# Row standard deviations on one core: the first group in eight transfers of 16 partitions, and four smaller changes to a kernel's two ends

## The chip, the core and the metric

The kernel runs on one core of a Trainium2 chip. Its time is the device time of one execution in microseconds (us), taken as the median of several executions. The profile of one execution has a span, from the first to the last instruction that the profiler saw; it is 1.7 to 2.1 us shorter than the device time. Engines are called TensorE, VectorE (DVE in the profile), ScalarE (ACT), GpSimdE (POOL) and SyncE (SP, which here only waits and issues transfers). "DMA engines" are the sixteen that move data between HBM and the on-chip memory SBUF.

## The reference

```python
def setup_inputs():
    return {"x": np.random.randn(8192, 8192).astype(np.float32)}

def reference(x):
    return np.std(x, axis=1)
```

The input has 268.4 MB, the output 32 KB. Every element is read once, so the load of x is the floor: at the 433.5 GB/s that the stream reaches below it is 619 us, an estimate (268.4 MB over that rate).

## The kernel before

The 8192 rows are cut into 30 groups of 256 rows and a tail of 512. A group is one transfer: partition p receives rows 2p and 2p+1, 64 KB in one piece, 8.39 MB in all. Three buffers are used in turn. For each group VectorE sums each row while ScalarE squares and sums it; the last groups and the tail are shared between the two engines by columns, so that the work left after the last byte is short. The last block of 128 rows arrives in pieces of columns.

```python
    pieces = [(3072, 768), (1536, 1024), (1024, 0), (1024, 512), (512, 0), (512, 0), (512, 0)]
    ...
    for g in range(G):                                            # G = 30
        if g >= NBUF:
            nc.sync.wait_ge(free, g - NBUF + 1)
        nc.sync.dma_start(out=buf[g % NBUF], in_=xg[g]).then_inc(lane[g % NBUF], 16)
    ...                                                           # the tail's transfers
    for g in range(G - 1):
        nc.vector.wait_ge(*landed(g))
        v_group.append(V.did(nc.vector.reduce_sum(                # row sums
            out=s_all[:, 2 * g:2 * g + 2],
            in_=buf[g % NBUF].rearrange("p (j m) -> p j m", j=2), axis=AX)))
    ...                                                           # ScalarE: squares
    shared(B0, ...); shared(B0 + 1, ...); shared(2 * G, ...)      # bn_stats + bn_aggr on VectorE
    ...
    q_groups = joined(vN[:, B0:2 * G], B0, 2 * G)                 # nine small GpSimdE operations
    ...
    aggregated(fin[:, 0:2], tri)                                  # the last block
    v_fin = V.did(nc.vector.transpose(out=tr, in_=fin[:, 1:33]))
    A.did(nc.scalar.activation(out=std_l, in_=tr, func=ACTF.Sqrt))
    A.need(A, A.n)
    nc.scalar.dma_start(out=out_l, in_=std_l[0:P:32, :]).then_inc(done_l, 16)
```

`landed(g)` is the semaphore value at which group g has arrived; every transfer adds 16.

Of the kernel before, what the change touches and what calls it, by code (L numbers as in the profile page):

```python
# [9 lines left out]
ALU = mybir.AluOpType  # L10
# [4 lines left out]
@with_exitstack  # L15
def kernel(
    ctx: ExitStack,
    tc: tile.TileContext,
    x: bass.AP,
    out: bass.AP,  # L20
):

    ctx.enter_context(tc.tile_critical())  # L23
    std_kernel(ctx, tc.nc, x, out)


def std_kernel(ctx, nc, x, out):
    P = nc.NUM_PARTITIONS
    R, C = x.shape
    N = float(C)  # L30
# [5 lines left out]
    TR = 4  # L36
    G = (R // P - TR) // 2
    B0 = 2 * (G - 1)
    T0 = 2 * G * P
    xg = x[0:T0, :].rearrange("(g p j) m -> g p (j m)", g=G, p=P, j=2)  # L40
    xt_rows = x[T0:R, :].rearrange("(t p) m -> t p m", p=P)
# [3 lines left out]
    out_l = out[T0:T0 + P].rearrange("(b i) -> b i", b=4)  # L45
    ACT_ROW = 3072
    N_D = float(C - ACT_ROW)
    H = C // 2
    pieces = [(3072, 768), (1536, 1024), (1024, 0), (1024, 512), (512, 0), (512, 0), (512, 0)]

    def sb(name, shape, dt=FP32):
        return ctx.enter_context(nc.sbuf_tensor(name, shape, dt))[:]

    def sem(name):
        return ctx.enter_context(nc.semaphore(name))

    NBUF = 3
    buf = [sb(f"x{i}", [P, 2 * C]) for i in range(NBUF)]

    dump = sb("dump", [P, C], mybir.dt.uint8)  # L60
    s_all = sb("s_all", [P, 2 * G + TR])
    q_all = sb("q_all", [P, 2 * G + TR])
    half = sb("half", [P, 2])
    agg = sb("agg", [P, 2 * G + TR - 1 - B0, 2])
    ident = sb("ident", [P, P])
    cinv = sb("cinv", [P, 1])
    nd = sb("nd", [P, 1])
    vN = sb("vN", [P, 2 * G])
    m2 = sb("m2", [P, 2 * G])
    u = sb("u", [P, TR])  # L70
    w = sb("w", [P, TR])
    t3 = sb("t3", [P, TR - 1])
    warm = sb("warm", [P, 1])

# [2 lines left out]
    std_l = sb("std_l", [P, 32])  # L77
# [24 lines left out]
    V = Line(nc.vector, "v")  # L102
    A = Line(nc.scalar, "a")
    Q = Line(nc.gpsimd, "q")
    T = Line(nc.tensor, "t")
    free, token, row_done, squared = sem("free"), sem("token"), sem("row_done"), sem("squared")
    lane = [sem(f"lane{i}") for i in range(NBUF)]
    NT = 4 + len(pieces)
    tail = [sem(f"tail{i}") for i in range(NT)]
    done_g, done_t, done_l = sem("done_g"), sem("done_t"), sem("done_l")  # L110

    def landed(g):
        return lane[g % NBUF], 16 * (g // NBUF + 1)

    xl, xa, xb = (buf[k % NBUF] for k in (G - 1, G, G + 1))



# [1 line left out]
        eng.addr_align(128, offset=0, max_nops=0)  # L120


    for g in range(G):
        if g >= NBUF:
            nc.sync.wait_ge(free, g - NBUF + 1)
        nc.sync.dma_start(out=buf[g % NBUF], in_=xg[g]).then_inc(lane[g % NBUF], 16)  # L126
    nc.sync.wait_ge(free, G - NBUF + 1)
    for i, t in enumerate((1, 2)):
        nc.sync.dma_start(out=xa[:, i * C:(i + 1) * C], in_=xt_rows[t]).then_inc(tail[i], 16)
    nc.sync.wait_ge(free, G - NBUF + 2)  # L130
    for h in range(2):
        nc.sync.dma_start(out=xb[:, h * H:(h + 1) * H],  # L132
                          in_=xt_rows[3][:, h * H:(h + 1) * H]).then_inc(tail[2 + h], 16)
    c0 = 0
    for i, (n, _) in enumerate(pieces):
        nc.sync.dma_start(out=xb[:, C + c0:C + c0 + n],
                          in_=xt_rows[0][:, c0:c0 + n]).then_inc(tail[4 + i], 16)
        c0 += n


    def q_op(op, *args, **kw):
        Q.need(Q, Q.n)
        return Q.did(op(*args, **kw))  # L143

    q_warm = Q.did(nc.gpsimd.memset(warm, 1.0))
    Q.did(nc.gpsimd.memset(ident, 1.0))
    q_op(nc.gpsimd.affine_select, out=ident, in_=ident, compare_op=ALU.is_equal,
                   fill=0.0, base=0, pattern=[[-1, P]], channel_multiplier=1)
    Q.did(nc.gpsimd.memset(cinv, 1.0 / N))
    Q.did(nc.gpsimd.memset(nd, N_D))  # L150
# [5 lines left out]
    v_group = []  # L156
    for g in range(G - 1):
        nc.vector.wait_ge(*landed(g))
        v_group.append(V.did(nc.vector.reduce_sum(  # L159
            out=s_all[:, 2 * g:2 * g + 2],  # L160
            in_=buf[g % NBUF].rearrange("p (j m) -> p j m", j=2), axis=AX)))

    def squash(src, n, func, acc, scale=1.0):
        A.need(A, A.n)
        return nc.scalar.activation(out=dump[:, 0:n], in_=src, func=func, scale=scale, accum_out=acc)  # L165
# [15 lines left out]
    for g in range(LOOPS * NBUF, G - 1):  # L181
        nc.scalar.wait_ge(*landed(g))
        for j in range(2):
            a_group[g] = A.did(squash(buf[g % NBUF][:, j * C:(j + 1) * C], C, ACTF.Square,
                                      q_all[:, 2 * g + j:2 * g + j + 1]))
    a_groups = A.n


    for g in range(G - 1):
        if g < LOOPS * NBUF:  # L190
            nc.tensor.wait_ge(*landed(g))
            nc.tensor.nop().then_inc(token, 1)
        T.need(V, v_group[g])
        if g in a_group:
            T.need(A, a_group[g])
        else:
            nc.tensor.wait_ge(squared, g + 1)
        nc.tensor.nop().then_inc(free, 1)  # L198


    def bn_cols(bn, k, src):
        n = src.shape[1]
        for d0 in range(0, n, F):
            V.did(nc.vector.bn_stats(out=bn[:, k * SD:(k + 1) * SD], in_=src[:, d0:min(n, d0 + F)]))  # L204
            k += 1
        return k

    def aggregated(out_ap, bn):
        V.need(V, V.n)
        return V.did(nc.vector.bn_aggr(out=out_ap, in_=bn))  # L210

    def shared(r, parts):
        bn = bns[r % 2]
        k = 0
        for i, (src, arrived) in enumerate(parts):
            a = ACT_ROW // len(parts)
            qa, sa = (q_all[:, r:r + 1], s_all[:, r:r + 1]) if i == 0 else (half[:, 1:2], half[:, 0:1])
            nc.scalar.wait_ge(*arrived)
            A.did(squash(src[:, 0:a], a, ACTF.Square, qa))
            A.did(squash(src[:, 0:a], a, ACTF.Copy, sa))  # L220
            nc.vector.wait_ge(*arrived)
            k = bn_cols(bn, k, src[:, a:src.shape[1]])
        aggregated(agg[:, r - B0, :], bn)

    def joined(out_ap, r0, r1):
        n = r1 - r0
        ndb = nd.to_broadcast((P, n))
        cb = cinv.to_broadcast((P, n))
        dm, dv = agg[:, r0 - B0:r1 - B0, 0], agg[:, r0 - B0:r1 - B0, 1]
        u_, w_ = u[:, 0:n], w[:, 0:n]  # L230
        q_op(nc.gpsimd.tensor_mul, u_, dm, dm)
        q_op(nc.gpsimd.tensor_add, u_, u_, dv)
        q_op(nc.gpsimd.tensor_mul, u_, u_, ndb)
        q_op(nc.gpsimd.tensor_add, u_, u_, q_all[:, r0:r1])
        q_op(nc.gpsimd.tensor_mul, w_, dm, ndb)
        q_op(nc.gpsimd.tensor_add, w_, w_, s_all[:, r0:r1])
        q_op(nc.gpsimd.tensor_mul, w_, w_, w_)
        q_op(nc.gpsimd.tensor_mul, w_, w_, cb)
        return q_op(nc.gpsimd.tensor_sub, out_ap, u_, w_)

    last = landed(G - 1)
    shared(B0, [(xl[:, 0:C], last)])
    shared(B0 + 1, [(xl[:, C:2 * C], last)])
    v_pair, a_pair = V.n, A.n
    shared(2 * G, [(xa[:, 0:C], (tail[0], 16))])


    Q.need(V, v_group[-1])
    Q.need(A, a_groups)
    q_op(nc.gpsimd.tensor_mul, m2[:, 0:B0], s_all[:, 0:B0], s_all[:, 0:B0])  # L250
    q_op(nc.gpsimd.tensor_mul, m2[:, 0:B0], m2[:, 0:B0], cinv.to_broadcast((P, B0)))
    q_op(nc.gpsimd.tensor_sub, vN[:, 0:B0], q_all[:, 0:B0], m2[:, 0:B0])
    Q.need(V, v_pair)
    Q.need(A, a_pair)
    q_groups = joined(vN[:, B0:2 * G], B0, 2 * G)


    vg = vN.rearrange("p (g j) -> p g j", j=2)
    T.need(Q, q_groups)
    for j in range(2):  # L260
        T.did(nc.tensor.transpose(ps_g[:, j, :], vg[:, :, j], ident))  # L261
    shared(2 * G + 1, [(xa[:, C:2 * C], (tail[1], 16))])
# [12 lines left out]
    c0, k, j = C, 0, 0  # L275
    for i, (n, a) in enumerate(pieces):
        src = xb[:, c0:c0 + n]
# [18 lines left out]
        k = bn_cols(tri[:, 3 * n_act:], k, src[:, a:n])  # L296
# [9 lines left out]
    v_fin = V.did(nc.vector.transpose(out=tr, in_=fin[:, 1:33]))  # L306
    A.need(V, v_fin)
    A.did(nc.scalar.activation(out=std_l, in_=tr, func=ACTF.Sqrt))  # L308
    A.need(A, A.n)
    nc.scalar.dma_start(out=out_l, in_=std_l[0:P:32, :]).then_inc(done_l, 16)  # L310
    nc.sync.wait_ge(done_g, 16)
    nc.sync.wait_ge(done_t, 16)
    nc.sync.wait_ge(done_l, 16)
# [30 lines left out]
```

## Time and profile before

| | before |
|---|---|
| median device time | 631.03 us (630.95 to 631.23, 3 runs) |
| span of the profile | 629.2 us |
| first transfer issued | 1.01 us |
| first row sum starts (group 0 has landed) | 23.41 us |
| one group to the next, landing to landing | 19.35 us (433.5 GB/s) |
| one row sum on VectorE | 17.22 us |
| last piece landed, last store landed | 624.02, 627.56 us |

The first lines are from the profile's page. The first two rows give the span in 40 equal slices: the busy tenths of the DMA engines (9 is 90% or more) and the GB/s that they moved. The third is the load queue: packets, MB, share of the sixteen engines' span.

```profile
DMA  9999999999999999999999999999999999999996
GB/s 401 400 467 400 467 400 467 400 462 404 462 404 462 404 467 400 467 400 467 400 467 400 467 400 467 400 467 400 467 400 467 400 467 400 467 400 467 400 422 247
...
q1 hardware_dynamic: 5955, 268.47, 98.9%
```

The stream is not idle until its end, and a group takes longer to arrive (19.35 us) than to be summed (17.22 us). The loads set the time, and only what happens before the stream runs, in it, or after its last byte can change it.

The timeline (start us, length us, engine, line, operation, output from input; in brackets the engine's idle time ahead of it and what ended that) shows the two ends.

```profile
1.01 1.35 SPq L126 DMA_DIRECT2D x<-in_x_dram  x3
...
23.41 17.22 DVE L159 TENSOR_REDUCE s_all<-x 128x2 f32<-128x16384 f32 x1 [23.41 <-DMA x<-in_x_dram]
...
623.75 0.27 SPq L302 DMA_DIRECT2D out_dram<-std_t  x1
...
624.85 0.52 DVE L210 BATCH_NORM_AGGREGATE fin<-tri 128x2 f32<-128x81 f32 x1
625.40 0.21 DVE L306 STREAM_TRANSPOSE tr<-fin 128x32 f32<-128x32 f32 x1
625.65 0.23 ACT L308 ACTIVATE std_l<-tr 128x32 f32<-128x32 f32 x1 [1.92 <-DVE tr L306]
625.91 1.11 ACTq L310 DMA_DIRECT2D out_dram<-std_l  x1
```

Two details of the trace's packet records: a group is 128 packets of 64 KB, eight for each DMA engine, and a packet in the running stream takes 2.42 us. The sixteen first packets begin at 2.04 to 3.10 us and end at 5.12 to 5.61 us.

### The profile page before, as it was taken

What the parts mean: (1) busy time and instruction counts of PE and PEld (TensorE: products, weight loads), DVE (VectorE), ACT (ScalarE), POOL (GpSimd) and SP (SyncE); (2) the same over time, 40 slices, a digit from 0 to 9 for tenths busy, and PEclk for the clock granted to TensorE, in tenths of its full rate; (3) what the DMA queues carried; (4) which work ended last, traced back from release to release, by engine and by line L of the source; (5) the groups of instructions that cost most, each with busy time, mean ns of one, the idle gap of its engine ahead of it and who ended that gap; (6) DMA issues with size and microseconds to landing.
All of it is one profiled execution on the core that took longest, in us unless ns stands there. A gap on an engine that the chain in (4) does not pass through costs nothing.

```text
span 629.2 us, 676 instructions
## 1 busy us (share of the span) xinstructions
PE 1.0 (0%) x3; PEld 0.2 (0%) x3; DVE 539.1 (86%) x98; ACT 450.1 (72%) x158; POOL 7.4 (1%) x45
## 2 busy tenths in 40 slices
PE   0000000000000000000000000000000000000000
PEld 0000000000000000000000000000000000000000
DVE  0588988889888889888898888998888988889897
ACT  0466876667866679766687666786667976768885
POOL 0000000000000000000000000000000000000012
DMA  9999999999999999999999999999999999999996
GB/s 401 400 467 400 467 400 467 400 462 404 462 404 462 404 467 400 467 400 467 400 467 400 467 400 467 400 467 400 467 400 467 400 467 400 467 400 467 400 422 247
DMA packets 5965, 268.49 MB, mean 427 GB/s; under 512 B 682, under 2 KB 715, under 8 KB 1483
## 3 DMA queue, kind: packets, MB, share of 16 engines
q1 hardware_dynamic: 5955, 268.47, 98.9%
q14 instruction: 2, 0.02, 0.0%
q10 hardware_dynamic: 8, 0.00, 0.0%
HBM read 268.44 MB, written 0.03 MB: 427 GB/s over the span
## 4 chain that ended last, share of the span: by engine, by line
DMA 70%; DVE 29%; SPq 0%; issue 0%; PEldq 0%; ACT 0%; DVEq 0%
DMA x<-in_x_dram 70%; DVE s_all L159 27%; DVE tri L204 1%; SPq L132 0%; PEldq L198 0%; DVE fin L210 0%; SPq L126 0%; ACT std_l L308 0%; DVE tr L306 0%; SPq L339 0%; DVEq L100 0%; SPq L23 0%
## 5 line engine op out<-in xcount | busy, mean ns | idle before, releaser
L159 DVE TENSOR_REDUCE s_all<-x 128x2 f32<-128x16384 f32 x29 | 499.4, 17220 | 83.2 <-DMA x<-in_x_dram 83.2
L165 ACT ACTIVATE dump<-x 128x8192 uint8<-128x8192 f32 (+5 forms) x76 | 440.8, 5800 | 172.5 <-ACTq L173 148.4
L204 DVE BATCH_NORM_STATS2 bn<-x 128x6 f32<-128x512 f32 x50 | 30.1, 675 | 2.8 <-DMA x<-in_x_dram 2.8
L165 ACT ACTIVATION_READ_ACCUMULATOR dump<-x (+1 forms) x76 | 14.2, 186 | 0.0
L204 DVE BATCH_NORM_STATS2 tri<-x 128x6 f32<-128x512 f32 (+1 forms) x12 | 7.1, 659 | 0.2 <-DMA x<-in_x_dram 0.2
L143 POOL TENSOR_TENSOR m<-s_all 128x58 f32<-128x58 f32 x1 | 0.3, 282 | 580.8 <-DVE s_all L159 580.8
L169 ACT ACT_TABLE_LOAD x1 | 1.3, 1283 | 1.4 <-SPq L23 1.4
L210 DVE BATCH_NORM_AGGREGATE agg<-bn 128x2 f32<-128x60 f32 x5 | 2.1, 426 | 0.2
L308 ACT ACTIVATE std_l<-tr 128x32 f32<-128x32 f32 x1 | 0.2, 229 | 1.9 <-DVE tr L306 1.9
L261 PE MATMUL ps_g<-ident,vN 128*30 128x128 f32 x2 | 0.6, 410 | 600.1 <-POOL vN L143 600.1
L210 DVE BATCH_NORM_AGGREGATE fin<-tri 128x2 f32<-128x81 f32 x1 | 0.5, 521 | 0.1
L143 POOL TENSOR_TENSOR m_p<-tri 128x1 f32<-128x1 f32 x3 | 0.6, 193 | 1.7 <-ACT dump L165 1.6
L143 POOL TENSOR_TENSOR tri<-q_p,m_p 128x1 f32<-128x1 f32 x3 | 0.6, 189 | 0.2
L143 POOL TENSOR_TENSOR m_p<-m_p,tri 128x1 f32<-128x1 f32 x3 | 0.6, 189 | 0.2
L143 POOL TENSOR_TENSOR u<-agg 128x2 f32<-128x2 f32 (+1 forms) x2 | 0.4, 192 | 14.0 <-DVE agg L210 13.9
L265 ACT ACTIVATE std_g<-ps_g 30x128 f32<-30x128 f32 x2 | 0.4, 256 | 0.0
L289 PE MATMUL ps_t<-ident,t 128*3 128x128 f32 x1 | 0.4, 376 | 19.8 <-POOL t L143 19.8
L143 POOL TENSOR_TENSOR s_all<-s_all,half 128x1 f32<-128x1 f32 x1 | 0.2, 189 | 17.5 <-DVE agg L210 17.5
L143 POOL TENSOR_TENSOR w<-w,cinv 128x2 f32<-128x2 f32 (+1 forms) x2 | 0.4, 196 | 0.2
L143 POOL TENSOR_TENSOR w<-w,s_all 128x2 f32<-128x2 f32 (+1 forms) x2 | 0.4, 196 | 0.2
L143 POOL TENSOR_TENSOR u<-u,nd 128x2 f32<-128x2 f32 (+1 forms) x2 | 0.4, 194 | 0.2
L143 POOL TENSOR_TENSOR u<-u,agg 128x2 f32<-128x2 f32 (+1 forms) x2 | 0.4, 193 | 0.2
(24 smaller groups left out, 4.7 us busy)
## 6 DMA issues: line engine op xcount, KB each, us to landing
x<-in_x_dram SPq DMA_DIRECT2D x2, 4096.0 KB, 35.7
x<-in_x_dram SPq DMA_DIRECT2D x2, 2048.0 KB, 28.6
x<-in_x_dram SPq DMA_DIRECT2D x1, 1536.0 KB, 34.1
x<-in_x_dram SPq DMA_DIRECT2D x2, 512.0 KB, 36.7
x<-in_x_dram SPq DMA_DIRECT2D x1, 768.0 KB, 35.5
x<-in_x_dram SPq DMA_DIRECT2D x3, 256.0 KB, 37.3
x<-in_x_dram SPq DMA_DIRECT2D x30, 40.7
out_dram<-std_g SPq DMA_DIRECT2D x1, 30.0 KB, 14.0
```

What stands on the lines that cost most here:

```text
L143: return Q.did(op(*args, **kw))
L159: v_group.append(V.did(nc.vector.reduce_sum(out=s_all[:, 2 * g:2 * g + 2], in_=buf[g % NBUF].rearrange("p (j m) -> p j m", j=2), axis=AX)))
L165: return nc.scalar.activation(out=dump[:, 0:n], in_=src, func=func, scale=scale, accum_out=acc)
L169: A.did(nc.scalar.activation(out=warm, in_=warm, func=ACTF.Sqrt))
L204: V.did(nc.vector.bn_stats(out=bn[:, k * SD:(k + 1) * SD], in_=src[:, d0:min(n, d0 + F)]))
L210: return V.did(nc.vector.bn_aggr(out=out_ap, in_=bn))
L261: T.did(nc.tensor.transpose(ps_g[:, j, :], vg[:, :, j], ident))
L265: a_std = A.did(nc.scalar.activation(out=std_g[:, :, j], in_=ps_g[:, j, :], func=ACTF.Sqrt, scale=1.0 / N))
L289: T.did(nc.tensor.transpose(ps_t, t3, ident))
L308: A.did(nc.scalar.activation(out=std_l, in_=tr, func=ACTF.Sqrt))
```

## The change

The intent is to shorten both ends: start the stream sooner with transfers that give each DMA engine one packet, issue the last store from SyncE, take a chain of small operations from GpSimdE to VectorE, let GpSimdE instead of SyncE lead the barriers (the points where all engines wait for one another) around the section so that SyncE can issue at once, and shrink the last piece. The core of the diff (helpers and renamed temporaries are cut):

```diff
-    ctx.enter_context(tc.tile_critical())
+    ctx.enter_context(tc.tile_critical(sync_engine=mybir.EngineType.Pool))
...
-    pieces = [(3072, 768), (1536, 1024), (1024, 0), (1024, 512), (512, 0), (512, 0), (512, 0)]
+    pieces = [(3072, 768), (1536, 1024), (1024, 0), (1024, 512), (512, 0), (512, 0), (256, 0), (256, 0)]
...
-        return lane[g % NBUF], 16 * (g // NBUF + 1)
+        return lane[g % NBUF], 16 * (g // NBUF + 1 + (P // 16 - 1) * (g % NBUF == 0))
...
-    for g in range(G):
+    S0 = P // 16
+    for k in range(S0):
+        load(buf[0][k:P:S0], xg[0][k:P:S0], lane[0])
+    for g in range(1, G):
...
+    V.need(A, a_groups)
+    v_op(nc.vector.scalar_tensor_tensor, out=m2[:, 0:B0], ...)       # two of 128x58
+    v_op(nc.vector.tensor_sub, vN[:, 0:B0], ...)
     shared(B0, ...); shared(B0 + 1, ...); shared(2 * G, ...)
-    ...                                   # twelve GpSimdE operations
+    ...                                   # six VectorE operations of 128x2
...
-    A.need(A, A.n)
-    nc.scalar.dma_start(out=out_l, in_=std_l[0:P:32, :]).then_inc(done_l, 16)
+    nc.sync.wait_ge(A.sem, A.n)
+    nc.sync.dma_start(out=out_l, in_=std_l[0:P:32, :]).then_inc(done_l, 16)
```

`buf[0][k:P:8]` (below `S0` is 8) are partitions k, k+8, k+16, ..., k+120: eight transfers of 1 MB each, which together fill all 128 partitions.

More of the change, by code (lines that the diff above doesn't have):

```diff
@@ L21 @@
 ):
-    ctx.enter_context(tc.tile_critical())
-    std_kernel(ctx, tc.nc, x, out)
-def std_kernel(ctx, nc, x, out):
+    ctx.enter_context(tc.tile_critical(sync_engine=mybir.EngineType.Pool))
+    nc = tc.nc
     P = nc.NUM_PARTITIONS
@@ L69, in std_kernel @@
     m2 = sb("m2", [P, 2 * G])
-    u = sb("u", [P, TR])
-    w = sb("w", [P, TR])
+    u, w, uq, wq = (sb(n, [P, TR]) for n in ("u", "w", "uq", "wq"))
     t3 = sb("t3", [P, TR - 1])
@@ L120, in std_kernel, with load @@
         eng.addr_align(128, offset=0, max_nops=0)
-    for g in range(G):
+    def load(dst, src, s):
+        nc.sync.dma_start(out=dst, in_=src).then_inc(s, 16)
+    S0 = P // 16
+    for k in range(S0):
+        load(buf[0][k:P:S0], xg[0][k:P:S0], lane[0])
+    for g in range(1, G):
         if g >= NBUF:
             nc.sync.wait_ge(free, g - NBUF + 1)
-        nc.sync.dma_start(out=buf[g % NBUF], in_=xg[g]).then_inc(lane[g % NBUF], 16)
+        load(buf[g % NBUF], xg[g], lane[g % NBUF])
     nc.sync.wait_ge(free, G - NBUF + 1)
     for i, t in enumerate((1, 2)):
-        nc.sync.dma_start(out=xa[:, i * C:(i + 1) * C], in_=xt_rows[t]).then_inc(tail[i], 16)
+        load(xa[:, i * C:(i + 1) * C], xt_rows[t], tail[i])
     nc.sync.wait_ge(free, G - NBUF + 2)
     for h in range(2):
-        nc.sync.dma_start(out=xb[:, h * H:(h + 1) * H],
-                          in_=xt_rows[3][:, h * H:(h + 1) * H]).then_inc(tail[2 + h], 16)
+        load(xb[:, h * H:(h + 1) * H], xt_rows[3][:, h * H:(h + 1) * H], tail[2 + h])
     c0 = 0
     for i, (n, _) in enumerate(pieces):
-        nc.sync.dma_start(out=xb[:, C + c0:C + c0 + n],
-                          in_=xt_rows[0][:, c0:c0 + n]).then_inc(tail[4 + i], 16)
+        load(xb[:, C + c0:C + c0 + n], xt_rows[0][:, c0:c0 + n], tail[4 + i])
         c0 += n
@@ L146, in std_kernel @@
     Q.did(nc.gpsimd.memset(ident, 1.0))
-    q_op(nc.gpsimd.affine_select, out=ident, in_=ident, compare_op=ALU.is_equal,
+    q_ident = q_op(nc.gpsimd.affine_select, out=ident, in_=ident, compare_op=ALU.is_equal,
                    fill=0.0, base=0, pattern=[[-1, P]], channel_multiplier=1)
@@ L229, in joined @@
         dm, dv = agg[:, r0 - B0:r1 - B0, 0], agg[:, r0 - B0:r1 - B0, 1]
-        u_, w_ = u[:, 0:n], w[:, 0:n]
+        u_, w_ = uq[:, 0:n], wq[:, 0:n]
         q_op(nc.gpsimd.tensor_mul, u_, dm, dm)
@@ L239, in joined, with v_op @@
         return q_op(nc.gpsimd.tensor_sub, out_ap, u_, w_)
+    def v_op(op, *args, **kw):
+        V.need(V, V.n)
+        return V.did(op(*args, **kw))
     last = landed(G - 1)
+    V.need(A, a_groups)
+    v_op(nc.vector.scalar_tensor_tensor, out=m2[:, 0:B0], in0=s_all[:, 0:B0], scalar=1.0 / N,
+         in1=s_all[:, 0:B0], op0=ALU.mult, op1=ALU.mult)
+    v_op(nc.vector.tensor_sub, vN[:, 0:B0], q_all[:, 0:B0], m2[:, 0:B0])
     shared(B0, [(xl[:, 0:C], last)])
     shared(B0 + 1, [(xl[:, C:2 * C], last)])
-    v_pair, a_pair = V.n, A.n
+    a_pair = A.n
     shared(2 * G, [(xa[:, 0:C], (tail[0], 16))])
-    Q.need(V, v_group[-1])
-    Q.need(A, a_groups)
-    q_op(nc.gpsimd.tensor_mul, m2[:, 0:B0], s_all[:, 0:B0], s_all[:, 0:B0])
-    q_op(nc.gpsimd.tensor_mul, m2[:, 0:B0], m2[:, 0:B0], cinv.to_broadcast((P, B0)))
-    q_op(nc.gpsimd.tensor_sub, vN[:, 0:B0], q_all[:, 0:B0], m2[:, 0:B0])
-    Q.need(V, v_pair)
-    Q.need(A, a_pair)
-    q_groups = joined(vN[:, B0:2 * G], B0, 2 * G)
+    V.need(A, a_pair)
+    dm, dv = agg[:, 0:2, 0], agg[:, 0:2, 1]
+    u_, w_ = u[:, 0:2], w[:, 0:2]
+    v_op(nc.vector.tensor_mul, u_, dm, dm)
+    v_op(nc.vector.tensor_add, u_, u_, dv)
+    v_op(nc.vector.scalar_tensor_tensor, out=u_, in0=u_, scalar=N_D, in1=q_all[:, B0:2 * G],
+         op0=ALU.mult, op1=ALU.add)
+    V.did(nc.vector.scalar_tensor_tensor(out=w_, in0=dm, scalar=N_D, in1=s_all[:, B0:2 * G],
+                                         op0=ALU.mult, op1=ALU.add))
+    v_op(nc.vector.scalar_tensor_tensor, out=w_, in0=w_, scalar=1.0 / N, in1=w_,
+         op0=ALU.mult, op1=ALU.mult)
+    v_groups = v_op(nc.vector.tensor_sub, vN[:, B0:2 * G], u_, w_)
     vg = vN.rearrange("p (g j) -> p g j", j=2)
-    T.need(Q, q_groups)
+    T.need(V, v_groups)
+    T.need(Q, q_ident)
     for j in range(2):
```

## The prediction

> **What bounds the kernel now.** The load stream. The page shows the DMA engines at 9 tenths in 39 of 40 slices, 268.49 MB, and one load queue with 98.9% of the 16 engines' span. The chain of waits puts loads plus the row sums that free their buffers on the chain, but a group lands every 19.35 us (23.38, 42.73, 62.09, ...; 433.5 GB/s) and a row sum takes 17.22 us, so only loads limit. The middle of the kernel does not change. What can move:
> - Start: SyncE issues the first load at 1.01 us; the packet records begin at 2.04 us on the first engine and 3.10 us on the last, and the first 64 KB packets end at 5.12 to 5.61 us. A steady packet takes about 2.42 us, so the streams effectively start at 2.7 to 3.2 us, 1.7 to 2.2 us after the issue.
> - End (timeline): last piece lands 624.02; its statistics 624.06 to 624.74; aggregate, transpose, square root to 625.88; store issued on ScalarE 625.91, issue takes 1.11 us, landed 627.56; closing barriers to 629.2.
>
> **Costs of the five parts.**
> 1. First group in 8 transfers. A transfer of 16 partitions gives each engine one 64 KB packet[...]. I estimate first packets from about 1.8 us and a stream 0.6 us earlier. [...] Seven extra completion packets per engine cost about 0.01 us each (records near the end): +0.08. SyncE issues every 0.46 us, a packet lasts 2.42, so no engine starves. Net -0.5 us, all critical.
> 2. Final store on SyncE. The three-partition store there took 0.27 us to issue and landed 1.13 us after issue began, against 1.65 for the last one on ScalarE. -0.5 us, all critical.
> 3. Combining on VectorE. Removes GpSimdE work that ends at 600.0 us, not critical. Adds two 128x58 operations into a 2.1 us idle stretch (free), and six 128x2 operations after 603.91. [...] each is about 0.16 us; with hand-over some 0.9 us in all. VectorE's idle before the next loads (0.25, 0.38, 0.17 us) absorbs nearly all of it; 0 to 0.1 us reaches the last pieces.
> 4. Last pieces of 256. VectorE works the last twelve statistics at 0.595 us spacing against landings 0.66 apart, nearly saturated. The last statistic shrinks from 0.68 to 0.41 us (a 256 took that), but one more fixed cost and one more transfer eat it: about 0, with the delay of part 3 possibly +0.1.
> 5. Section led by GpSimdE. SyncE no longer leads the entry: its first issue perhaps 0.05 us earlier. The exit has the same hops: 0 +- 0.1.
>
> **Sum.** 631.03 - 0.5 - 0.5 - 0.05 + 0.05 = about 630.0 us, range 629.3 to 630.7. Faster by over 2%: 0.005; within 2%: 0.95; slower by over 2%: 0.045.
>
> **What would show it.** First packets end about 4.7 us and group one lands near 22.9; period still 19.35 us; last store issued on SyncE lands about 1.1 us after issue; six VectorE operations of about 0.16 us, VectorE then without idle until the end; exit barriers about 1.6 us as before.
>
> **What would make it wrong.** [...] the first group takes about twice 19.3 us and the kernel some 19 us more[...]. Otherwise: [...] a dearer exit.

The marked cuts take out grounds that no trace or run of this case shows: why smaller transfers should start sooner, why an operation of 128x2 should take 0.16 us (the changed kernel's six then took 0.155 to 0.161), why 16 partitions 8 apart might load at half speed, and two other risks. No term of the sum is cut: 631.03 - 0.5 - 0.5 - 0.05 + 0.05 us makes 630.03, about 630.0. Its first -0.5 us is the stream's 0.6 us less 0.08 for completion packets. The 0.6 us and the 1.8 us beside it were estimates. That 16 partitions get one packet for each of sixteen engines is seen in the changed kernel's packet records: eight transfers of 16 packets, in sixteen chains of eight.

## The result

| | before | after |
|---|---|---|
| median device time | 630.99 us (4 runs) | 651.62 us (651.38 to 651.85, 4 runs) |
| ratio | | 1.0326, 95% interval 1.0308 to 1.0344 |
| span | 629.2 | 649.7 |
| first row sum starts | 23.41 | 44.69 |
| from there to the last piece landed | 600.61 | 600.36 |
| last piece landed to last store landed | 3.54 | 3.47 |
| last store landed to end of span | 1.69 | 1.19 |

A ratio is the mean time of one kernel's runs over that of the other's in the same rounds, so not quite the ratio of the medians quoted. Executions over 1.5% slower than the fastest of the same kernel are left out of the means. The last four rows add up to the two spans; their differences are +21.28, -0.25, -0.07 and -0.50 us, together the 20.46 us by which the span grew. The change is slower, and the whole loss lies ahead of the first row sum. Here are the page's rows and the timeline of the changed kernel that answer to those of before.

```profile
DMA  9999999999999999999999999999999999999996
GB/s 195 198 307 399 452 452 391 448 452 440 399 452 452 391 448 452 440 399 452 452 391 448 452 440 399 452 452 395 444 452 444 395 452 452 395 444 452 414 417 269
...
q1 hardware_dynamic: 6219, 268.47, 99.0%
```

```profile
0.95 6.27 SPq L121 DMA_DIRECT2D x<-in_x_dram  x10
...
44.69 17.22 DVE L161 TENSOR_REDUCE s_all<-x 128x2 f32<-128x16384 f32 x1 [44.69 <-DMA x<-in_x_dram]
...
644.69 0.26 SPq L316 DMA_DIRECT2D out_dram<-std_t  x1
...
645.83 0.55 DVE L212 BATCH_NORM_AGGREGATE fin<-tri 128x2 f32<-128x87 f32 x1
646.41 0.21 DVE L320 STREAM_TRANSPOSE tr<-fin 128x32 f32<-128x32 f32 x1
646.65 0.23 ACT L322 ACTIVATE std_l<-tr 128x32 f32<-128x32 f32 x1 [1.99 <-DVE tr L320]
646.91 0.60 SPq L324 DMA_DIRECT2D out_dram<-std_l  x1
```

The row of busy tenths is the same as before, and the queue's share went up, from 98.9 to 99.0%. It says that the DMA engines always held a packet, not that packets moved at full speed. The row below it shows what happened: the first two slices moved 195 and 198 GB/s, about half. The windows say it again, here before, then after (columns: window, length, busy time and count of PE and PEld, which are TensorE's multiplies and weight loads, of DVE, ACT and POOL, then the clock, DMA share, GB/s).

```profile
2.00:23.00 21.00, 0.00 (x0) 0.00 (x0) 0.00 (x0) 0.91 (x2) 0.00 (x0) 1.00 1.07 450
23.00:45.00 22.00, 0.00 (x0) 0.00 (x0) 19.46 (x2) 16.23 (x5) 0.00 (x0) 1.00 0.99 429
```

```profile
2.00:23.00 21.00, 0.00 (x0) 0.00 (x0) 0.00 (x0) 0.86 (x2) 0.00 (x0) 1.00 1.15 241
23.00:45.00 22.00, 0.00 (x0) 0.00 (x0) 0.32 (x1) 0.05 (x1) 0.00 (x0) 1.00 0.88 200
```

(A packet is counted whole where it begins, so a short window can show a little too much or too little.) In the packet records, all sixteen engines are at work from the start, and their 64 KB packets take 5.11 us (median) instead of 2.42 us, until the eighth; after one mixed round at the start of group 1 it is 2.42 us again, and groups land 19.34 us apart. Eight packets for each engine, each longer by 2.69 us, make 21.5 us: that is the whole loss of 21.3 us.

### The profile page after: what moved, and what is told of

Same layout as the page of the kernel before. It is cut to its first block, busy times and chain, and to the rows that moved or that the text cites. A ratio compares the mean times of both kernels' runs of the same rounds, so it can differ in the third digit from the quotient of the medians.

```text
span 649.7 us, 684 instructions
## 1 busy us (share of the span) xinstructions
PE 1.0 (0%) x3; PEld 0.2 (0%) x3; DVE 540.2 (83%) x107; ACT 450.1 (69%) x158; POOL 4.8 (1%) x33
## 4 chain that ended last, share of the span: by engine, by line
DMA 62%; DVE 35%; SPq 1%; another core or an unknown queue 1%; issue 0%; PEldq 0%; ACT 0%; DVEq 0%; POOLq 0%
DMA x<-in_x_dram 62%; DVE s_all L161 29%; DVE bn L206 5%; DVE tri L206 1%; SPq L121 1%; DVE agg L212 0%; PEldq L200 0%; DVE fin L212 0%; DVE u L245 0%; ACT std_l L322 0%; DVE tr L320 0%; DVE w L245 0%; DVE vN L245 0%; DVE w L264 0%
```

## The experiments

Four theories of the loss were on the table, and the runs were chosen to part them:

- **Set of partitions.** How long a packet takes depends on which partitions a transfer reaches. For each set the author had a forecast, drawn from an account of why that no trace or run of this case shows. The account is cut from the recorded texts, with its name where it headed a forecast; the figures without a theory's name stay as forecasts alone, to be held against the runs.
- **Small transfers.** Transfers that give an engine one packet each, with a completion after it, cannot overlap.
- **Source.** Reading rows 512 KB apart in HBM at once is slow.
- **Something else in the change,** with the split first group as a bystander.

The cuts of code below leave out what only follows from an edit, such as the count in `landed`.

### Undo the split: e1_one_load

```diff
-    for k in range(S0):
-        load(buf[0][k:P:S0], xg[0][k:P:S0], lane[0])
-    for g in range(1, G):
+    for g in range(G):
```

> The changed kernel with the first group loaded by one transfer again; the other four parts of the change stay. If the split first group is the whole loss (all theories of it), the first group lands near 23.4 us again and the kernel takes 630.2 to 630.6 us: the span minus the 21.3 us by which group one landed later in the changed kernel (44.69 against 23.41). If the other parts cost something of their own, it is above 631.

Measured: 630.78 us (630.66 to 630.89, 5 runs), a little above the 630.2 to 630.6 expected; ratio 0.9996 (0.9982 to 1.0010). The first row sum starts at 23.58 us:

```profile
23.58 17.22 DVE L158 TENSOR_REDUCE s_all<-x 128x2 f32<-128x16384 f32 x1 [23.58 <-DMA x<-in_x_dram]
```

The loss is gone; what stays of the other four parts is 0.2 us of gain by the medians, within the interval of none.

### The split alone: e2_split_only

```diff
-    for g in range(G):
+    for k in range(8):
+        nc.sync.dma_start(out=buf[0][k:P:8], in_=xg[0][k:P:8]).then_inc(lane[0], 16)
+    for g in range(1, G):
```

> The kernel before with the split first group alone. All theories of the split: 651.5 to 652.5 us, first row sum starting near 44.7 us. If the loss needed another part of the change as well (GpSimdE leading the section, the order of the first issues), well under 650.

Measured: 651.77 us (651.71 to 651.88, 4 runs), ratio 1.0329 (1.0313 to 1.0345); the first row sum starts at 44.48 us:

```profile
44.48 17.22 DVE L162 TENSOR_REDUCE s_all<-x 128x2 f32<-128x16384 f32 x1 [44.48 <-DMA x<-in_x_dram]
```

The split first group alone makes the loss. The fourth theory is out.

### Neighbouring partitions: e3_16_neighbours

```diff
-        load(buf[0][k:P:S0], xg[0][k:P:S0], lane[0])
+        load(buf[0][16 * k:16 * k + 16], xg[0][16 * k:16 * k + 16], lane[0])
```

> The changed kernel with each of the 8 transfers on 16 neighbouring partitions in place of 16 partitions 8 apart. [...] a 64 KB packet takes about 4 x 2.42 = 9.7 to 10.2 us, the first group lands near 80 to 84 us, the kernel takes 687 to 692 us. Theory 'small transfers' (a transfer of one packet for each engine, with a completion packet after each, cannot overlap): packets of 5.1 us as with 8 apart, 651.6 us. Theory 'source' (rows 512 KB apart in HBM are slow to read together): the rows are now neighbours, so packets of 2.42 us and about 631 us.

Measured: 685.17 us (2 runs), ratio 1.0858. Its timeline:

```profile
0.95 4.77 SPq L121 DMA_DIRECT2D x<-in_x_dram  x10
...
77.94 17.22 DVE L161 TENSOR_REDUCE s_all<-x 128x2 f32<-128x16384 f32 x1 [77.94 <-DMA x<-in_x_dram]
```

The same count of transfers of the same size is a further 33 us slower when their partitions are neighbours, and the HBM rows were neighbours too, so neither "source" nor "small transfers" explains it as they were stated. The forecast for the set of partitions, the first in the expectation, had the order and the size nearly right: packets took 9.3 us, a little less than the 9.7 to 10.2 us expected. (Of its "4 x 2.42", the 2.42 us is measured.)

### Eight ways of loading: p1_patterns

The kernel before loads its first group eight more times at the start, each time another way, each after the one ahead has landed. The whole edit is these loops, with a wait after each:

```diff
+    dma(B, X)                                                     # 1: one transfer
+    for k in range(8): dma(B[k:P:8], X[k:P:8])                    # 2: 16 partitions, 8 apart
+    for k in range(8): dma(B[16*k:16*k+16], X[16*k:16*k+16])      # 3: 16 neighbours
+    for k in range(7): dma(B[k:k+106:7], X[k:k+106:7])            # 4: 16 partitions, 7 apart
+    for k in range(8): dma(B[k:P:8], X[16*k:16*k+16])             # 5: as 2, neighbouring source rows
+    for k in range(4): dma(B[k:P:4], X[k:P:4])                    # 6: 32 partitions, 4 apart
+    for k in range(8): dma(B[:, 2048*k:2048*k+2048], X[:, ...])   # 7: 128 partitions, 1 MB by columns
+    for k in range(2): dma(B[64*k:64*k+64], X[64*k:64*k+64])      # 8: 64 neighbours
```

> The kernel before, with the first group loaded eight more times ahead of its own load, each way after the one ahead has landed; the result stays right. Each way is read by the time of its 64 KB packets and from its first issue to its last landing; one whole transfer takes about 21 to 22 us. [...] (1) one transfer of 128: 2.42 us packets, 19.3 us of packets; (2) 8 of 16, 8 apart: 5.1 us, 39 to 41 us; (3) 8 of 16 neighbours: about 10 us, 77 to 82 us; (4) 7 of 16, 7 apart[...]: mixed 2.4 and 4.8 to 5.1, about 21.7 us of packets; (5) 16 partitions 8 apart filled from 16 neighbouring rows: as (2); (6) 4 of 32, 4 apart: [...]; (7) 8 transfers of 128 partitions by 8 KB, 1 MB each as in (2): no loss, about 20 us; (8) 2 of 64 neighbours: [...]. Theory 'small transfers': (2), (3), (4), (5) all 5.1 us packets, so (4) takes 36 us; (7), as many transfers of as many bytes, slow too. Theory 'source': (5) fast, 2.42 us packets, and (3) fast.

The figures ahead of "Theory 'small transfers'" are those for the set of partitions. Ways 6 and 8 had two each, 39 and 19.3 us, for two ways in which a transfer's partitions might be dealt to the engines.

The first columns are worked from the issue lines (first issue to last landing), the packets from the packet records:

| way | first issue to last landing | a 64 KB packet, median |
|---|---|---|
| 1: one transfer of 128 | 22.2 us | 2.42 us |
| 2: 8 of 16, 8 apart | 43.1 | 5.10 |
| 3: 8 of 16 neighbours | 76.5 | 9.28 |
| 4: 7 of 16, 7 apart (7/8 of the bytes) | 33.2 | 4.67 |
| 5: as 2, source rows neighbours | 43.1 | 5.09 |
| 6: 4 of 32, 4 apart | 22.2 | 2.42 |
| 7: 8 of 128 by columns, 1 MB each | 22.3 | (8 KB) 0.31 |
| 8: 2 of 64 neighbours | 43.2 | 5.12 |

And these are the windows in the middle of the eight ways, in that order.

```profile
2.00:22.00 20.00, 0.00 (x0) 0.00 (x0) 0.00 (x0) 0.92 (x2) 0.00 (x0) 1.00 1.00 420
26.00:64.00 38.00, 0.00 (x0) 0.00 (x0) 0.00 (x0) 0.00 (x0) 0.00 (x0) 1.00 0.94 193
69.00:138.00 69.00, 0.00 (x0) 0.00 (x0) 0.00 (x0) 0.00 (x0) 0.00 (x0) 1.00 0.95 106
146.00:172.00 26.00, 0.00 (x0) 0.00 (x0) 0.00 (x0) 0.00 (x0) 0.00 (x0) 1.00 1.00 242
178.00:216.00 38.00, 0.00 (x0) 0.00 (x0) 0.00 (x0) 0.00 (x0) 0.00 (x0) 1.00 0.94 193
222.00:240.00 18.00, 0.00 (x0) 0.00 (x0) 0.00 (x0) 0.00 (x0) 0.00 (x0) 1.00 0.94 408
243.00:262.00 19.00, 0.00 (x0) 0.00 (x0) 0.00 (x0) 0.00 (x0) 0.00 (x0) 1.00 1.01 423
266.00:304.00 38.00, 0.00 (x0) 0.00 (x0) 0.00 (x0) 0.00 (x0) 0.00 (x0) 1.00 0.94 193
```

Read the last two columns against each other: the DMA share is 0.94 to 1.01 in every line, while GB/s goes from 106 to 423. Way 7 moves as many bytes in as many transfers as way 2 and loses nothing, and way 6 splits by partitions and loses nothing: the size of a transfer is not the cause. (In these two an engine still gets eight packets or two from a transfer; the case of exactly one is in p2 and p3 below.) Way 5 loses as much as way 2 from other source rows: the source is not. What goes with the loss is the set of partitions: 16 neighbours moved 106 GB/s, 64 neighbours 193, 16 partitions 8 apart 193, 32 partitions 4 apart 408. (These are windows of a queue; sixteen packets of 64 KB in their time, 9.28, 5.12 and 2.42 us, are 113, 205 and 433 GB/s.)

Ways 6 and 8 each came near one of their two expectations: way 6 ran at full speed, 22.2 us from first issue to last landing as the one transfer of 128, and way 8 at half, 43.2 us. How their partitions are dealt to the engines, neither shows. Way 4 missed: it was expected at 21.7 us of packets, part of them at 2.4 us; nearly all packets took 4.7 us. In its fourth and fifth transfer most took about 3.4 us. The next two tests followed that up.

### More ways: p2_patterns and p3_seven_apart

The same form with other loops; in p2: two transfers of 64 partitions 2 apart; four of 32 neighbours; 16 partitions 7 apart from partition 3, three times; the same from partition 0; 16 partitions 4 apart in each half; 16 partitions 5 apart. In p3: 7 apart from partitions 1, 2, 4, 5 and 6, three times each.

```diff
+    for k in range(3): dma(buf[k][3:109:7], X[3:109:7])     # p2, third; p3 with 1, 2, 4, 5, 6
```

> The kernel before with more ways of loading ahead of its own first load, as in the other test of patterns; packets are 64 KB. [...] (1) 2 transfers of 64 partitions 2 apart: [...]; (2) 4 of 32 neighbours: at least 5.1 us[...]; (3) 7 apart from partition 3, three times[...]: two engines at 4.8, the others faster, about 3.4 us as in the first test's third and fourth transfers; (4) 7 apart from partition 0[...]: 4.7 us as in its first transfers; (5) 8 of 16 partitions 4 apart in each half[...]: 5.1 us; (6) 16 partitions 5 apart[...]: about 4.8 us. Theory 'only the number of packets a transfer gives an engine matters': (3) to (6) all 5.1 us, (2) 2.42 us as with 32 partitions 4 apart.

> The kernel before with, ahead of its own first load, three transfers of 16 partitions 7 apart from partition 1, then three from 2, from 4, from 5 and from 6. [...] from 4 two engines at 4.8 us a packet and fourteen at 2.42; from the others four at 4.8 and twelve at 2.42. [...] from 4 as above, from the others all sixteen at 4.7 to 4.95.

In p2's expectation way 1 had two forecasts, 2.42 and 5.1 us, and way 2 a second one of 9.3 us. In p3's, two rivals stand one after the other: from 1, 2, 5 and 6 either four engines are slow or all sixteen; from 4 both forecast two.

Packets of p2: 64 partitions 2 apart 2.42 us; 32 neighbours 5.11; 7 apart from 3: two engines at 4.82 to 4.83 and fourteen at 2.42 (second packets); 7 apart from 0: all sixteen at 4.93; 4 apart in each half 5.09; 5 apart 4.8 to 5.0, all sixteen. Windows of p2 for the first and second way:

```profile
4.00:22.00 18.00, 0.00 (x0) 0.00 (x0) 0.00 (x0) 0.00 (x0) 0.00 (x0) 1.00 0.94 408
26.00:64.00 38.00, 0.00 (x0) 0.00 (x0) 0.00 (x0) 0.00 (x0) 0.00 (x0) 1.00 0.94 193
```

Packets of p3, second of the three: from 4, two engines at 4.83 and fourteen at 2.42; from 1, 2, 5 and 6 all sixteen at 4.91 to 5.03. The second rival is right.

"Small transfers" ends here: these transfers give each engine exactly one packet, as the changed kernel's do, and fourteen engines ran at 2.42 us. (The expectation had put these fourteen near 3.4 us.)

The starts from 3 and from 4 are the cleanest evidence that the set of partitions makes the loss: transfers of one count, size and step have two slow engines of sixteen there (4.82 to 4.83 us), and sixteen from 0, 1, 2, 5 and 6 (4.91 to 5.03 us). The records do not name an engine's partition, so which partitions the two slow engines served is not shown, nor what decides between two and sixteen. For the changed kernel it makes no difference: all 128 packets of its first group were slow (4.18 to 5.21 us). Also open is why they take 5.11 us where twice 2.42 would be 4.84 us.

### A split that avoids the loss: f1_four_of_32

```diff
-    S0 = P // 16
+    S0 = P // 32          # 4 transfers of 32 partitions, 4 apart; landed() counts 4
```

> The changed kernel whole, with the first group in 4 transfers of 32 partitions 4 apart in place of 8 of 16 partitions 8 apart. [...] as in the kernel with one load, 630.6 to 631.0 us, first row sum near 23.7 us, packets of 2.42 us. Theory 'any split by partitions costs': above 640 us.

Measured: 630.64 us (630.58 to 630.87, 4 runs), ratio 0.9994 (0.9979 to 1.0009). The whole changed kernel, still with a split first group, is at the kernel before's time:

```profile
0.96 3.92 SPq L121 DMA_DIRECT2D x<-in_x_dram  x6
...
23.35 17.22 DVE L161 TENSOR_REDUCE s_all<-x 128x2 f32<-128x16384 f32 x1 [23.35 <-DMA x<-in_x_dram]
```

Splitting the group by partitions is not what costs; the choice of partitions is.

### The four smaller parts, one at a time

Here "leads" means: runs the barriers around the section.

```diff
# s1: the last store on SyncE        s2: sync_engine=mybir.EngineType.Pool
# s3: pieces ..., (512, 0), (512, 0), (256, 0), (256, 0)
# s4: e1 with the store on ScalarE, SyncE leading, last pieces of 512
```

> The kernel before with the last store issued by SyncE, nothing else. The prediction: 0.5 us faster (630.5), since the 3-partition store there landed 1.13 us after its issue began. The profiles of the changed kernel and of the one with a single first load say otherwise: this store's issue took 0.59 us on SyncE and it landed 1.61 us after its issue began, against 1.65 us on ScalarE. So 630.95, no gain.

> The kernel before with GpSimdE leading the section, nothing else. The prediction: first issue 0.05 us earlier, exit unchanged, 630.95. Read from the profile with a single first load: first issue at 0.95 in place of 1.01 us, and from the end of the last wait to the end of the span 1.13 us in place of 1.64. So if the lead is the cause of both, 630.5 to 630.7 by the clock and a span near 628.7.

> The kernel before with last pieces of 512, 512, 256, 256 columns, nothing else. The prediction: about 0. VectorE is nearly saturated by then: the last statistic ends at the same time or 0.1 us later; 630.95 to 631.1.

> The changed kernel's combining on VectorE alone; first group in one transfer, last store on ScalarE, SyncE leading, last pieces of 512. The prediction: six operations of about 0.16 us after the third aggregate, 0.9 us with hand-over, of which 0 to 0.1 us reaches the end: 631.0 to 631.1. A rival: it lengthens the end by all that VectorE is delayed at the third tail block, 0.8 us: 631.8.

| alone | median of 5 | ratio, 95% interval | store issue to landing | store landed to span end |
|---|---|---|---|---|
| before | 630.94 (9 runs) | | 1.65 us | 1.69 us |
| s1 store on SyncE | 631.16 | 1.0003 (0.9989 to 1.0016) | 1.63 | 1.69 |
| s2 GpSimdE leads | 630.74 | 0.9998 (0.9984 to 1.0011) | 1.66 | 1.47 |
| s3 pieces of 256 | 631.21 | 1.0006 (0.9992 to 1.0020) | 1.66 | 1.69 |
| s4 combining on VectorE | 630.70 | 0.9997 (0.9983 to 1.0011) | 1.66 | 1.32 |

No interval leaves out 1, so by the clock none of the four is shown to do anything; the profiles, one each, show where tenths went. The store on SyncE takes a little over half as long to issue (0.61 us against 1.11), and lands no sooner:

```profile
626.16 0.61 SPq L310 DMA_DIRECT2D out_dram<-std_l  x1
```

GpSimdE's lead and the twelve operations taken from GpSimdE each go with a shorter exit (from the last store's landing to the end of the span), by 0.22 and 0.37 us, in one profile each; s2's span of 629.3 us is above the 628.7 us expected if the lead alone made the exit shorter. The seven profiled kernels with both parts have an exit of 1.17 to 1.19 us; with the end of before it was 1.69 to 1.72 us in six profiles and 2.25 us in one (p2). Most of this does not reach the clock: device time less span is 2.0 us (median) in the kernels with both parts that were run more than once and 1.7 us in the others, so 0.3 of the 0.5 us comes back outside the span, where no profile looks. Combining cost what was predicted: the six operations take 0.15 or 0.16 us each and VectorE reaches the next statistics 0.8 us late (lines of e1_one_load, three of the six),

```profile
603.51 0.43 DVE L209 BATCH_NORM_AGGREGATE agg<-bn 128x2 f32<-128x60 f32 x1
604.04 0.16 DVE L242 TENSOR_TENSOR u<-agg 128x2 f32<-128x2 f32 x1
...
604.51 0.15 DVE L261 SCALAR_TENSOR_TENSOR w<-agg,s_all 128x2 f32<-128x2 f32 x1
...
604.89 0.16 DVE L242 TENSOR_TENSOR vN<-u,w 128x2 f32<-128x2 f32 x1
604.97 1.28 DVE L203 BATCH_NORM_STATS2 bn<-x 128x6 f32<-128x512 f32 x2
```

but the last statistic still ended 0.72 us after the last landing (s4: 624.61 after 623.89), as before (624.74 after 624.02). s4's median lies 0.3 us below the 631.0 to 631.1 us expected. Tenths of this size also drown in differences at the start: in the packet records of before, one DMA engine carries an 8 KB instruction fetch at 5.14 us, its load packet then takes 2.95 us in place of 2.42, and the first group's last completion comes 0.4 us after the next to last. Between the profiles of the kernels with an unslowed first group, the first row sum starts anywhere from 23.35 to 23.81 us.

### Why the store gained nothing: s5_store_4_neighbours, b1_best, g1_row_store

```diff
# all three on top of e1; s5 is wrong on purpose
-    nc.sync.dma_start(out=out_l, in_=std_l[0:P:32, :]).then_inc(done_l, 16)
+    nc.sync.dma_start(out=out_l, in_=std_l[0:4, :]).then_inc(done_l, 16)
# b1: no transpose, last pieces of 512
+    A.did(nc.scalar.activation(out=std_l[:, 0:1], in_=fin[:, 1:2], func=ACTF.Sqrt))
+    nc.sync.dma_start(out=<128 outputs as 128x1>, in_=std_l[:, 0:1]).then_inc(done_l, 16)
# g1: the row by TensorE, last pieces of 512
+    T.did(nc.tensor.transpose(ps_f, fin[:, 1:2], ident))
+    A.did(nc.scalar.activation(out=std_f, in_=ps_f, func=ACTF.Sqrt))
+    nc.sync.dma_start(out=out_t[0:1], in_=std_f).then_inc(done_l, 16)
```

> Wrong result on purpose in 128 of the 8192 outputs: the kernel with one first load, its last store reading 4 neighbouring partitions in place of 4 partitions 32 apart. If the step between partitions is what made this store's issue 0.59 us in place of 0.27 us, the issue takes 0.27 us and it lands about 1.15 to 1.3 us after its issue began in place of 1.62. If the count of 4 partitions or the 128-byte rows are, it stays at 0.59 and 1.6 us.

s5 gave a wrong result, as intended. Its store took 0.25 us to issue and landed 1.12 us after its issue began:

```profile
626.01 0.25 SPq L321 DMA_DIRECT2D out_dram<-std_l  x1
```

Count, bytes and rows of the store are the same as in e1 and the changed kernel (0.60 us to issue, landed after 1.62 us); only the distance between the source partitions, 1 instead of 32, differs. The distance was worth the 0.5 us that the prediction had booked for the engine, in one profile.

> An attempt to beat both: one load for the first group, last pieces of 512, combining on VectorE, GpSimdE leading, and the last store made from a 128x1 column straight after the aggregate, without the transpose of 0.22 us and its hand-over. Against the kernel before: 0.2 us from lead and combining, 0.25 us from the transpose, less what 128 stores of 4 bytes take more than 4 of 128: 630.3 to 630.8 us.

b1 missed badly: 636.10 us (635.61 to 636.48, 5 runs), ratio 1.0080. The store in its timeline, and then, from the waits of SyncE's queue (in total, times, longest us), the wait for it:

```profile
625.58 0.36 SPq L319 DMA_DIRECT2D out_dram<-std_l  x1
```

```profile
SPq L322 <- DMA out_dram<-std_l: 6.7, 1, 6.7
```

128 stores of 4 bytes landed 7.1 us after the issue began (632.68), where four rows of 128 bytes had taken 1.6 us. The transpose that it saved took 0.21 us.

> A correct attempt to beat both: one first load, last pieces of 512, and the last block's result turned into one row by TensorE (about 0.4 us and a hand-over, against 0.22 us on VectorE) and stored from one partition as one row of 512 bytes. If the distance between the partitions is what cost the last store 0.35 us of issue and 0.5 us to landing, this one's issue takes about 0.27 us and lands 1.1 to 1.2 us after; less 0.25 us for TensorE, 0.2 us under the kernel with one first load: 630.3 to 630.7 us.

g1 is right and the fastest kernel measured: 630.41 us (630.18 to 630.57, 5 runs) beside 631.06 us (630.77 to 631.16, 9 runs), ratio 0.9990 (0.9976 to 1.0003). Each of its runs is under each run of before, though the interval does not leave out 1. Its end:

```profile
625.03 0.52 DVE L211 BATCH_NORM_AGGREGATE fin<-tri 128x2 f32<-128x81 f32 x1
...
625.61 0.37 PE L319 MATMUL ps_f<-ident,fin 128*1 128x128 f32 x1 [4.19 <-DVE fin L211]
626.02 0.27 ACT L321 ACTIVATE std_f<-ps_f 1x128 f32<-1x128 f32 x1 [2.08 <-PE ps_f L319]
626.31 0.23 SPq L323 DMA_DIRECT2D out_dram<-std_f  x1
```

The store as one row was issued in 0.23 us, and it had landed at 627.38 us, 1.07 us after the issue began.

## Why the prediction was wrong

The step that failed is the first of the five, "First group in 8 transfers ... SyncE issues every 0.46 us, a packet lasts 2.42, so no engine starves. Net -0.5 us, all critical." It took the duration of a packet from transfers of 128 partitions and carried it to transfers of 16. The packets lasted 5.11 us. e2, f1 and p1 show that the set of partitions makes this (in p1 16 partitions 8 apart 5.10 us, 32 partitions 4 apart 2.42). The step measured +21.3 us in place of -0.5 us. That no engine starves was right; what was wrong is the 2.42 us.

Its smaller half was wrong as well. "First packets from about 1.8 us": they began at 2.36 to 3.43 us, later than before's 2.04 to 3.10. A transfer of 16 partitions 8 apart took 0.57 to 0.72 us to issue, against 0.41 us for one of 128, and its first packet began 1.40 us after the issue, against 1.03 us. The split in four, which has no slow packets, began no sooner (2.31 us) and gained nothing over one load that the clock can tell. Nor did the 16 neighbours of e3 begin sooner: 0.39 to 0.62 us to issue and 1.02 us to the first packet, much as the one load of 128 in e1 (0.42 and 1.04 us). So a smaller transfer bought no earlier start in any of these three, and with partitions 8 apart the first packet came some 0.4 us later.

The prediction did name what then happened, with its size ("some 19 us more"), and gave a loss of over 2% a chance of 4.5%. Nothing in before's profile spoke for so low a chance: every load there covers 128 partitions, so no record told what another set would do.

Point by point for the rest:

- **What bounds the kernel** (loads; groups 19.35 us apart): right; 19.34 us after.
- **Store on SyncE, -0.5 us**: wrong, nothing measured. The 1.13 us that was carried over belonged to a store from three neighbouring partitions; this one reads partitions 32 apart, with an issue of 0.60 us and a landing after 1.62 us. s5 shows that the distance is the difference.
- **Combining on VectorE, six of 0.16 us, 0 to 0.1 us at the end**: right on both. The six operations took 0.153 to 0.161 us.
- **Pieces of 256, about 0**: right as far as measured.
- **Lead**: the first issue at 0.95 in place of 1.01 us, as predicted; the exit was 0.5 us shorter in the changed kernel, which was not, though the clock gained less (see s2 and s4).

Without the split, the sum of the other four was predicted at about -0.5 us and came out at -0.2 us by the medians (e1), with an interval that includes no change.

## What to carry to other kernels

A duration measured on one set of partitions is shown for that set alone (here 2.42 us a packet on 128 partitions, 5.11 on 16 that are 8 apart): before splitting a transfer by partitions, time a packet of the new set, as p1 does with a few loads ahead of the kernel, and prefer splits that keep the rate (here by columns, 32 partitions 4 apart or 64 partitions 2 apart: 408 to 423 GB/s in p1 and p2). A DMA row full of nines only says that packets are in flight (the same nines stood over 195 GB/s and over 400 to 467); read GB/s or the time of a packet beside it. The partitions matter for a store of a few bytes too, where the distance between them was worth more than the engine that issued it (0.5 us to landing in s5, nothing in s1).

## What was measured, by set of partitions

- A 64 KB packet took 2.42 us in one transfer of 128 partitions, in four of 32 partitions 4 apart and in two of 64 partitions 2 apart (408 GB/s in the windows of the last two); 5.09 to 5.12 us with 16 partitions 8 apart, 16 partitions 4 apart in each half, 32 neighbours and 64 neighbours (193 GB/s in the windows of 8 apart, 32 and 64 neighbours), 4.8 to 5.0 us with 16 partitions 5 apart; 9.28 us with 16 neighbours (106 GB/s).
- With 16 partitions 7 apart all sixteen engines were slow in five starts (4.91 to 5.03 us a packet); in two starts two engines were (4.82 to 4.83 us) and fourteen took 2.42 us. In p1's fourth and fifth transfer of way 4 most took about 3.4 us.
- Transfers of 16 partitions did use sixteen engines (sixteen chains of packets at once in the changed kernel's first group). How the partitions of a transfer of 32 or 64 are dealt to them is not shown.
- An issue on SyncE took 0.25 us for 4 neighbouring partitions, 0.33 to 0.42 for most of 128, 0.42 (median) for 16 neighbours, about 0.6 for 16 that are 8 apart or 4 that are 32 apart; the last also landed 0.5 us later than from neighbours. On ScalarE that one took 1.11 us.
- A store of 128 times 4 bytes landed 7.1 us after its issue began, one of 512 bytes after 1.07 us.
